# The first part of a gated DeltaNet mixer in another order: logit weights split earlier, decays behind the third convolution, convolutions apart from heads

## The chip, the core and the metric

One core of one Trainium2 chip runs the whole kernel in one launch. The metric is the device time of an execution in microseconds (us); a kernel's time is the median of its runs. The kernel before was run three times: 1945.94 us median, 1945.79 us lowest, 1953.51 us highest.

## What is computed

One inference step of a two-layer decoder trunk on 544 tokens: a prompt of 512 and eight samples of 4 tokens each, with shared weights, model width 1024, all in float32. Each layer is half an FFN, a mixer, half an FFN, each behind an RMS norm and added to the residual. Layer 0 mixes with stick-breaking attention and an RG-LRU; layer 1, the "odd" one, is a gated DeltaNet with 8 heads of width 128. Only the odd mixer matters here:

```python
def deltanet_mixer(u, conv_buf, S0, w_in, conv_w, A_log, dt_bias, o_gain, w_out):
    proj = u @ w_in                                   # 1024 -> q, k, v, z (1024 each), 8 + 8 logits
    qkv, z, b_logit, a_logit = jnp.split(proj, ...)
    qkv, new_buf = causal_conv(conv_buf, qkv, conv_w) # width 4, per channel
    q, k, v = jnp.split(jax.nn.silu(qkv), 3, axis=-1)
    q = l2_normalize(q) * (DN_HEAD_DIM ** -0.5); k = l2_normalize(k)
    beta = jax.nn.sigmoid(b_logit)
    g = -jnp.exp(A_log) * jax.nn.softplus(a_logit + dt_bias)
    o, S = gated_delta_chunked(q, k, v, beta, g, S0)  # G = cumsum(g); decay = exp(G_i - G_j); A = k k^T * decay * beta; ...
    o = rms_norm(o, o_gain) * jax.nn.silu(z)
    return o @ w_out, (new_buf, S)
```

## The kernel before

**Linear layers.** The activations lie feature-major, 128 features on the partitions and 544 tokens along the free axis, in two halves of 256 and 288 columns. Every linear layer (`mm3`, L347) is made of float32r matmuls: weights and activations are each split into a high and a low part and three products are added up (L362 to L364), so one 128-column tile of weights over 1024 inputs takes 48 matmuls for both halves. The weights of such a tile (class `W`, L304) come by one DMA of 512 KB on SyncE's queue (L319) into `raw` (two buffers); ScalarE rounds it to `wh` (L323, three buffers), VectorE subtracts to get `wl` (L324, two buffers). The product stands in a PSUM bank of tag `lin`, of which the odd mixer has two; the bank comes free when VectorE has read it (L1068 for the first half of a convolution, L1071 and L1072 for the second).

**Which order counts.** The Python code traces the instructions in one order, and a planner of the tile framework gives each engine its fixed order at build time: of the instructions that its own cost model holds to be ready, the one traced first. Each engine's queue then runs in that order on the chip, whatever comes late. The tokens of `ODD_ORDER` (L903) set the traced order of the odd mixer.

**Where layer 1's FFN meets the mixer.** `ffn_body` ends with eight feature tiles; behind each of them `split_x` makes the mixer's inputs `xh` (ScalarE, L267) and `xl` (VectorE, L268) and adds up the squares (`xsq`, L271 and L273). The weights that come next are loaded and split meanwhile. `mid` is a hook between the two linear layers of the FFN, in which `odd_consts` (L945) loads the mixer's constants.

**The start of the mixer.** `norm_stats` makes `rstd`, the tokens' scale (L280 to L289). `odd_setup` (L984) takes the 16 columns of logit weights as one more `W`, multiplies (48 matmuls, 16 output rows), scales the two halves by `rstd` into `bt` (L991), transposes them to tokens (L995), computes beta and the decays in many small steps (softplus with ScalarE's exponential at L100, five small matmuls L1018 to L1022, running sums `G`), writes `G` to DRAM (L1050, L1051) and reads it back as rows that are repeated on every partition (`grs` L1053; `grow`, and in `xsq` for the odd head, L1108).

**Heads.** The heads go in four groups of two. Token D (`decays`) makes for both heads of a group the two decay matrices `Dn` and `Dt`: 16 VectorE instructions of 128 x 128 (L1113, L1114) and their exponentials on ScalarE. Token H (`head_stage`, L1122) makes a head's q and k with `conv_tile` (L1056: linear layer, a scaled copy on ScalarE L1080, three multiply-adds on VectorE L1082, SiLU on ScalarE), then transposes (L1132, L1138), squares (L1134, L1140) and the products k k^T and q k^T (L1151, L1159) that the decays weight (L1153, L1160). These four PSUM results are of tag `m`, which has two banks. Token B makes v with a third `conv_tile`, Z the gate, V, L, S, C, R the inverse, the chunks' chain and the samples, O and M the output layer.

**Function tables.** ScalarE's exponential and its SiLU lie in different table sets. `E.table` (L86) issues a load of the other set where the set changes (L91) and orders it behind every traced use of the last set and ahead of every use of the next. Copies and squares are bound to no set.

```python
ODD_ORDER = "D0 H0 H1 B0 B1 V0 Z0 L0 Z1 S0 C0 R0 D2 H2 B2 H3 B3 ..."
...
    qT = conv_tile(E, op, w_in, 0, h, sq)      # in head_stage
    kT = conv_tile(E, op, w_in, 1, h, sq)
...
        norm_stats(E)                          # in odd_mixer
        odd_setup(E, cp, op, w_in)
        odd_heads(E, op, dp, w_in, w_out, nxt)
```

Of the kernel before, what the change touches and what calls it, by code (L numbers as in the profile page):

```python
# [15 lines left out]
P = 128  # L16
D = 1024
# [58 lines left out]
class Env:  # L76
# [75 lines left out]
def fetch_vectors(E, part):  # L152
    """Small vectors as rows of 128: the norms' gains, or the rest."""
# [46 lines left out]
def fetch_x(E, io, first):  # L200
    """The tokens' rows on their way, the norms' gains among them."""
# [13 lines left out]
def load_x(E, gname):  # L215
    """x feature-major and its split parts, the first half of the tokens ahead of the second."""
# [27 lines left out]
def store_tile(E, m, y, ys):  # L244
    """The output's columns of one feature tile, by way of the rows y and ys."""
# [58 lines left out]
class W:  # L304
    """Weight rows ks (of 128) by some columns, at most 8 blocks of 128 x 128, split in two exact float32r parts."""
# [22 lines left out]
    def part(self, c0, cn):  # L328
        """The columns c0 and on alone."""
# [5 lines left out]
def wide(E, src, ks):  # L335
    """Weight rows ks, all columns: a list of 128-column parts, each made when it is asked for."""
# [10 lines left out]
def mm3(E, ws, xh, xl, evac, ks=None, halves=(0, 1)):  # L347
    """psum[cols, half] = W^T x with three exact products."""
    nc = E.nc
    for h in halves:  # L350
# [8 lines left out]
        for i, (w, k) in enumerate(terms):  # L359
# [4 lines left out]
            nc.tensor.matmul(ps[:n], lhsT=wl, rhs=rh, start=False, stop=(i == len(terms) - 1))  # L364
# [67 lines left out]
def softplus_exp(E, pool, x, n):  # L432
    """exp(-|x|), the part of softplus that takes ScalarE's exponential."""
# [6 lines left out]
def softplus_log(E, pool, out, x, e, n):  # L440
    """out = softplus(x) = max(x, 0) + log1p(e), e = exp(-|x|), the logarithm by the series of atanh."""
# [21 lines left out]
def even_consts(E, cp):  # L463
# [36 lines left out]
    # gather rows of the pages in reverse: pool row page * 128 + 127 - p, four row parts each  # L500
# [54 lines left out]
def lru_gate_weights(E):  # L555
    """The gates' 64 x 64 blocks, two of them on the diagonal of each [128, 128]; exact float32r parts."""
# [103 lines left out]
def to_tokens(E, src, dst, sdst, dram, sdram, p):  # L660
    """Feature-major [128, NT] to token rows, kept in dst / sdst and stored."""
# [49 lines left out]
def page(E, ap, name, o):  # L711
    """A page of the cache, its rows in reverse."""
# [6 lines left out]
def sample_scores(E, ap, qb, ks, zs, hf):  # L719
    """q k of the sample's heads, rows (b in 4, head, token): 256 past keys in reverse, then the new ones."""  # L720
# [23 lines left out]
def sample_weights(E, ap, zs):  # L744
# [13 lines left out]
    for hf in range(2):  # L758
        nc.vector.tensor_tensor_scan(t[:, hf, :256], E.ones256, m[:, hf, :256], tot[:, hf:hf + 1], op0=ALU.mult, op1=ALU.add)
# [143 lines left out]
ODD_ORDER = "D0 H0 H1 B0 B1 V0 Z0 L0 Z1 S0 C0 R0 D2 H2 B2 H3 B3 Z2 Z3 V2 L2 D4 S2 C2 R2 H4 H5 B5 D6 Z4 B4 V4 Z5 H6 S4 H7 B6 L4 V6 C4 R4 B7 Z6 O0 Z7 N L6 C6 S6 R6 M2 O6"  # L903
# [21 lines left out]
def rsqrt_small(E, out, m, shape, tag):  # L925
    """out = m^-1/2 on a few columns: a first guess from the exponent, then Newton's steps."""
# [13 lines left out]
def bc(ap, n):  # L940
    """[p, a] -> [p, a, n], the last dimension repeated."""
# [3 lines left out]
def odd_consts(E, op):  # L945
# [14 lines left out]
    # conv weights and states, channels on partitions  # L960
# [17 lines left out]
    E.ogain = gc  # L978
    E.ad = op.tile([P, 2, NH], F32, name="ad")
# [63 lines left out]
    # the decays as rows, by way of DRAM, repeated on every partition  # L1043
# [12 lines left out]
def conv_tile(E, op, w_in, i, h, sq):  # L1056
    """Linear, causal convolution and SiLU of one 128-channel tile; the sample's tokens go to sq."""
# [23 lines left out]
    for j in range(1, 4):  # L1081
        nc.vector.scalar_tensor_tensor(a, XP[:, j:j + XW - 3], cw[j], a, op0=ALU.mult, op1=ALU.add)  # L1082
# [21 lines left out]
def head_decay(E, op, h):  # L1104
# [17 lines left out]
def head_stage(E, op, w_in, h, H, ssq, adr, sq):  # L1122
    """Everything of a head that does not need the inverse."""
# [3 lines left out]
    qT = conv_tile(E, op, w_in, 0, h, sq)  # L1127
    kT = conv_tile(E, op, w_in, 1, h, sq)
# [78 lines left out]
def levels(E, op, Hs, tdr):  # L1207
    """The transposed inverses of the 128 x 128 blocks of a group from those of their 32 x 32 blocks."""
# [430 lines left out]
```

## Time and profile before

| | us |
|---|---|
| runs: median, lowest, highest | 1945.94, 1945.79, 1953.51 |
| profiled execution, first to last instruction (span) | 1943.3 |
| median of the runs less that span | 2.6 |
| TensorE busy in the span | 1899.1 (98%) |
| VectorE busy | 1066.3 (55%) |
| ScalarE busy | 824.0 (42%) |
| mean granted TensorE clock | 0.989 |
| layer 1's odd mixer, from its first matmul | 1215.6 on |

The profiled execution has no run time of its own among the runs shown; its span is 2.6 us under their median, which holds the start and end of an execution that the span leaves out. Times in the rows are us from the span's start. The granted clock is a share of the full 2.4 GHz: 1.00 is 2.4 GHz, 0.50 is 1.2 GHz. "Busy" of PE (TensorE) is modelled for pipelined matmuls, so a busy PE may still be slow; where matmuls follow each other, the distance of their starts is what one costs. A wait names the instruction that ended it.

### The profile page before, as it was taken

The numbers are of one execution on the slowest core, as the hardware profiler recorded it, in microseconds if no ns is written. First come the engines' busy times: TensorE is split into PE (matmuls) and PEld (weight loads), VectorE is DVE, ScalarE is ACT, GpSimd is POOL, SyncE is SP. The second block draws the span as 40 slices with busy tenths as digits, with TensorE's granted clock in tenths as the row PEclk, the third lists the DMA queues.
The fourth block names the chain that finished last, engine by engine and source line by source line (L and its number), as shares of the span: only waits on it lengthen the run. The fifth ranks groups of instructions, "written<-read, shape, count | busy, mean of one in ns | idle before, by whom it ended". The sixth has DMA issues, their size and how long they took to land.

```text
span 1943.3 us, 36239 instructions
## 1 busy us (share of the span) xinstructions
PE 1899.1 (98%) x14905; PEld 1803.1 (93%) x14905; DVE 1066.3 (55%) x2544; ACT 824.0 (42%) x1709; POOL 110.9 (6%) x222
## 2 busy tenths in 40 slices
PE   7999999999999999999999999899999999999999
PEld 7999999879667999999999999799998998999998
DVE  7444335566755544433544433787968868444422
ACT  6333224667653433322433322566665636333221
POOL 0000001001221000000000000112110100000000
PEclk9999999999999999999999999999998999999999
DMA  4333233222323333323333323333343322333332
GB/s 132 87 88 88 80 90 98 78 55 84 93 84 91 88 87 87 88 83 88 99 88 87 88 80 79 88 96 92 92 108 86 92 79 69 87 88 88 88 110 67
DMA packets 313857, 171.00 MB, mean 88 GB/s; under 512 B 24310, under 2 KB 308166, under 8 KB 313692
## 3 DMA queue, kind: packets, MB, share of 16 engines
q1 hardware_dynamic: 311132, 160.30, 29.5%
q0 software_dynamic: 2560, 8.39, 1.5%
q8 instruction: 117, 1.92, 0.4%
q14 instruction: 48, 0.39, 0.1%
HBM read 158.01 MB, written 10.65 MB: 87 GB/s over the span
## 4 chain that ended last, share of the span: by engine, by line
PE 87%; DVE 5%; ACT 3%; issue 2%; DMA 2%; POOL 1%; SPq 0%; ACTq 0%; DVEq 0%; POOLq 0%
PE lin L362 25%; PE lin L363 25%; PE lin L364 25%; PE pv L707 1%; PE z L685 1%; DVE wl L324 1%; PE s L1421 1%; PE sc L736 1%; ACT wh L323 1%; PE po L783 0%; DMA raw<-in_w_ffn_in 0%; DVE acc L1082 0%; DVE ltmp L1199 0%; PE m L590 0%; ACT xh L267 0%
## 5 line engine op out<-in xcount | busy, mean ns | idle before, releaser
L362 PE MATMUL lin<-xh,wh 128*128 128x256 f32 (+2 forms) x2992 | 875.2, 293 | 18.5 <-DVE x L1532 4.2
L363 PE MATMUL lin<-xl,wh 128*128 128x256 f32 (+2 forms) x2992 | 872.8, 292 | 0.3 <-DVE xl L268 0.2
L364 PE MATMUL lin<-xh,wl 128*128 128x256 f32 (+2 forms) x2992 | 868.6, 291 | 1.2 <-DVE wl L324 1.2
L362 PEld LDWEIGHTS lin<-xh,wh 128*128 128x128 f32 (+1 forms) x2992 | 567.0, 190 | 25.3 <-ACT wh L323 6.4
L364 PEld LDWEIGHTS lin<-xh,wl 128*128 128x128 f32 (+1 forms) x2992 | 568.2, 190 | 9.2 <-issue 6.3
L363 PEld LDWEIGHTS lin<-xl,wh 128*128 128x128 f32 (+1 forms) x2992 | 567.4, 190 | 4.9 <-issue 2.3
L323 ACT ACTIVATE wh<-raw 128x1024 fp32r<-128x1024 f32 x261 | 275.6, 1057 | 507.5 <-PE lin L363 432.6
L324 DVE TENSOR_TENSOR wl<-raw,wh 128x1024 fp32r<-128x1024 f32 x261 | 317.2, 1215 | 89.6 <-PE lin L364 88.0
L362 PE MATMUL lin<-hh,wh 128*128 128x288 f32 (+1 forms) x1024 | 295.7, 289 | 0.0
L363 PE MATMUL lin<-hl,wh 128*128 128x288 f32 (+1 forms) x1024 | 295.4, 288 | 0.0
L364 PE MATMUL lin<-hh,wl 128*128 128x288 f32 (+1 forms) x1024 | 294.9, 288 | 0.0
L363 PEld LDWEIGHTS lin<-hl,wh 128*128 128x128 f32 x1024 | 193.0, 188 | 0.2
L364 PEld LDWEIGHTS lin<-hh,wl 128*128 128x128 f32 x1024 | 192.7, 188 | 0.1
L362 PEld LDWEIGHTS lin<-hh,wh 128*128 128x128 f32 x1024 | 192.5, 188 | 0.1
L401 DVE TENSOR_TENSOR sg<-lin,rstd 128x256 f32<-128x256 f32 (+1 forms) x128 | 55.9, 438 | 161.9 <-PE lin L364 161.9
L406 DVE TENSOR_TENSOR pr<-lin,rstd 128x256 f32<-128x256 f32 (+1 forms) x128 | 56.5, 441 | 155.3 <-PE lin L364 155.1
L370 ACT ACTIVATE hh<-pr 128x256 fp32r<-128x256 f32 (+1 forms) x128 | 55.1, 431 | 203.3 <-DVE pr L407 203.0
L423 DVE SCALAR_TENSOR_TENSOR x<-lin,x 128x256 f32<-128x256 f32 x64 | 28.2, 441 | 168.8 <-PE lin L364 168.8
L371 DVE TENSOR_TENSOR hl<-pr,hh 128x256 fp32r<-128x256 f32 (+1 forms) x128 | 56.6, 442 | 61.5 <-ACT hh L370 61.5
L100 ACT ACTIVATE sg<-sg 128x256 f32<-128x256 f32 (+1 forms) x128 | 53.7, 422 | 55.9 <-DVE sg L401 55.9
L267 ACT ACTIVATE xh<-x,vec 128x544 fp32r<-128x544 f32 (+2 forms) x64 | 39.6, 632 | 71.9 <-DVE x L423 59.6
L1082 DVE SCALAR_TENSOR_TENSOR acc<-XP,cw,acc 128x568 f32<-128x568 f32 x72 | 58.7, 816 | 3.9 <-ACT acc L1080 3.6
(474 smaller groups left out, 2056.4 us busy)
## 6 DMA issues: line engine op xcount, KB each, us to landing
raw<-in_w_ffn_in SPq DMA_DIRECT2D x128, 512.0 KB
raw<-in_w_ffn_out SPq DMA_DIRECT2D x64, 512.0 KB
raw<-in_w_in_odd SPq DMA_DIRECT2D x32, 512.0 KB
raw<-in_w_in_even SPq DMA_DIRECT2D x20, 512.0 KB
raw<-in_w_out_even SPq DMA_DIRECT2D x8, 512.0 KB
S<-in_state_dn_S SPq DMA_DIRECT2D x8, 512.0 KB
out_dn_S_sample<-S SPq DMA_DIRECT2D x8, 512.0 KB
raw<-in_w_out_odd SPq DMA_DIRECT2D x8, 512.0 KB
```

The lines of the kernel that those rows point to most:

```text
L100: i = self.nc.scalar.activation(out, in_, func, **kw).ins
L267: nc.scalar.activation(xh, x, AF.Copy, scale=g)
L323: nc.scalar.activation(self.h, raw, AF.Copy)
L324: nc.vector.tensor_tensor(self.l, raw, self.h.bitcast(F32), op=ALU.subtract)
L362: nc.tensor.matmul(ps[:n], lhsT=wh, rhs=rh, start=(i == 0), stop=False)
L363: nc.tensor.matmul(ps[:n], lhsT=wh, rhs=rl, start=False, stop=False)
L364: nc.tensor.matmul(ps[:n], lhsT=wl, rhs=rh, start=False, stop=(i == len(terms) - 1))
L370: nc.scalar.activation(yh, src, AF.Copy)
L371: nc.vector.tensor_tensor(yl, src, yh.bitcast(F32), op=ALU.subtract)
L401: nc.vector.tensor_tensor(s, ps, E.rstd[:, c0:c0 + cn], op=ALU.mult)
L406: nc.vector.tensor_tensor(p_, ps, E.rstd[:, c0:c0 + cn], op=ALU.mult)
L1082: nc.vector.scalar_tensor_tensor(a, XP[:, j:j + XW - 3], cw[j], a, op0=ALU.mult, op1=ALU.add)
```

## The change

Five things change; comments and docstrings that the diff also removes are left out here.

1. The logit weights are no longer a `W` of the mixer. `odd_consts` loads and splits them in the FFN's `mid` into tiles of their own (`w16`), so they take no `raw`, `wh` and `wl` buffer.
2. `odd_setup` is cut in two. `odd_logits` (the 48 matmuls and `bt`) stays at the start. The rest is token Y behind the first convolution; its first transpose is ordered behind the last matmul traced before it (`E.last_mm`, of q0).
3. Convolutions have tokens of their own: q0, k0, q1 and k1 are traced apart from H0 and H1, as "q0 Y k0 q1 D0 k1 H0 H1"; every other head takes its convolutions in its H token as before.
4. The first `Dn` instruction of heads 0 and 1 is ordered behind the last multiply-add of the convolution traced before (q1).
5. `ones256` shrinks to 128 columns and the samples' scan (L759) reads one column repeated 256 times; of three scratch tiles `junk` two stay.

Tokens q, k, Y and D each call `E.table`, so the sets now follow each other as SiLU (q0), exponential (Y), SiLU (k0, q1), exponential (D0), SiLU (k1 and on), where before there was one change behind D0.

```diff
-    E.ones256 = E.cp.tile([P, 256], F32, name="ones256")
-    nc.vector.memset(E.ones256, 1.0)
-    ones = E.ones256[:, :P]
+    ones = E.cp.tile([P, P], F32, name="ones")
+    nc.vector.memset(ones, 1.0)
...
-            nc.tensor.matmul(ps[:n], lhsT=wl, rhs=rh, start=False, stop=(i == len(terms) - 1))
+            E.last_mm = nc.tensor.matmul(ps[:n], lhsT=wl, rhs=rh, start=False, stop=(i == len(terms) - 1)).ins
...
-        nc.vector.tensor_tensor_scan(t[:, hf, :256], E.ones256, m[:, hf, :256], tot[:, hf:hf + 1], op0=ALU.mult, op1=ALU.add)
+        nc.vector.tensor_tensor_scan(t[:, hf, :256], E.ones[:, :1].to_broadcast([P, 256]), m[:, hf, :256], tot[:, hf:hf + 1], op0=ALU.mult, op1=ALU.add)
...
-ODD_ORDER = "D0 H0 H1 B0 B1 V0 Z0 L0 ...
+ODD_ORDER = "q0 Y k0 q1 D0 k1 H0 H1 B0 B1 V0 Z0 L0 ...
...
+    E.w16 = object.__new__(W)                                   # in odd_consts
+    raw = E.f()[:, :16 * KD].rearrange("p (k c) -> p k c", k=KD)
+    nc.sync.dma_start(out=raw, in_=w_in[:, 4096:4112].rearrange("(k p) c -> p k c", p=P))
+    E.w16.h, E.w16.l = (op.tile([P, KD, 16], F32R, name=n) for n in ("wh16", "wl16"))
+    split_to(E, E.w16.h, E.w16.l, raw)
+    E.w16.at = {k: k for k in range(KD)}
...
-def odd_setup(E, op, sp, w_in):
-    w = W(E, w_in[:, 4096:4112])
+def odd_logits(E, sp):
+    nc = E.nc
     bt = sp.tile([P, 4 * GH, P], F32, tag="V", name=E.nm("bt")).rearrange("p a b -> p (a b)")[:, :NT]
     def ev(h, c0, cn, ps):
         nc.vector.tensor_tensor(bt[:16, c0:c0 + cn], ps[:16], E.rstd[:16, c0:c0 + cn], op=ALU.mult)
-    mm3(E, [w], E.xh, E.xl, ev)
+    mm3(E, [E.w16], E.xh, E.xl, ev)
+    return bt
+
+def odd_setup(E, op, sp, bt):
     ps = E.m([P, 5, 16])
     for t, (c0, n) in enumerate(TOKS):
-        nc.tensor.transpose(ps[:n, t], bt[:16, c0:c0 + n], E.ident[:16, :16])
+        i = nc.tensor.transpose(ps[:n, t], bt[:16, c0:c0 + n], E.ident[:16, :16]).ins
+        if t == 0:
+            E.after(i, E.last_mm)
...
-        nc.vector.scalar_tensor_tensor(a, XP[:, j:j + XW - 3], cw[j], a, op0=ALU.mult, op1=ALU.add)
+        E.last_conv = nc.vector.scalar_tensor_tensor(a, XP[:, j:j + XW - 3], cw[j], a, op0=ALU.mult, op1=ALU.add).ins
...
-        nc.vector.scalar_tensor_tensor(Dn[:, c], ch(grow)[:, c], g, E.mba, op0=ALU.subtract, op1=ALU.max)
+        i = nc.vector.scalar_tensor_tensor(Dn[:, c], ch(grow)[:, c], g, E.mba, op0=ALU.subtract, op1=ALU.max).ins
+        if h < GH and c == 0:
+            E.after(i, E.last_conv)
...
-    qT = conv_tile(E, op, w_in, 0, h, sq)                       # head_stage now gets qT and kT
-    kT = conv_tile(E, op, w_in, 1, h, sq)
...
+    bt = odd_logits(E, op)                                      # in odd_heads
+
+    def linear(i, h):
+        g0 = h // GH * GH
+        if g0 not in st:
+            st[g0] = H = Group()
+            H.sq = op.tile([P, GH, 3, NS], F32, tag="sq", name=E.nm("sq"), bufs=2)
+        if (i, h) not in conv:
+            E.table("silu_and_others")
+            conv[i, h] = conv_tile(E, op, w_in, i, h, st[g0].sq)
+        return conv[i, h]
...
+        qT, kT = linear(0, h), linear(1, h)                     # in head(h)
+        head_stage(E, op, h, H.hs[h % GH], qT, kT, H.ssq, H.adr)
...
+        if c == "q":
+            linear(0, i)
+        elif c == "k":
+            linear(1, i)
+        elif c == "Y":
+            E.table(LNEXP)
+            odd_setup(E, cp, op, bt)
```

## Rows read from the trace of the kernel before

**Rows 1.** The page's first part, the whole span: busy time, share and instructions of each engine.

```profile
PE 1899.1 (98%) x14905; PEld 1803.1 (93%) x14905; DVE 1066.3 (55%) x2544; ACT 824.0 (42%) x1709; POOL 110.9 (6%) x222
```

**Rows 2.** The view of waits, PE alone, 1215 to 1262 us: who waited for whom, us in total, times, longest.

```profile
PE lin L362 <- DVE XP L1068: 3.7, 1, 3.7
PE m L995 <- DVE bt L991: 2.0, 1, 2.0
PE lin L362 <- ACT xh L267: 0.7, 1, 0.7
```

**Rows 3.** The table by stretches at the mixer's start: length, busy time and instructions of PE, PEld, DVE, ACT and POOL, granted clock, DMA share, GB/s. The sum is over the five stretches.

```profile
1223.50:1225.60 2.10, 0.14 (x2) 0.05 (x1) 1.91 (x6) 1.44 (x3) 0.00 (x0) 1.00 0.00 0
1225.60:1246.30 20.70, 20.70 (x160) 19.78 (x160) 15.92 (x56) 5.20 (x13) 3.82 (x8) 1.00 0.46 111
1246.30:1250.00 3.70, 0.00 (x0) 0.00 (x0) 3.70 (x13) 3.50 (x6) 0.00 (x0) 0.84 0.01 4
1250.00:1255.00 5.00, 4.96 (x23) 5.00 (x24) 2.71 (x8) 3.36 (x7) 3.18 (x5) 0.50 0.31 70
1255.00:1262.00 7.00, 6.96 (x52) 6.49 (x51) 4.93 (x15) 5.18 (x23) 0.57 (x3) 0.95 0.22 67
sum 38.50, PE 32.77 PEld 31.30 DVE 29.17 ACT 18.67 POOL 7.57; mean PE 6.55 PEld 6.26 DVE 5.83 ACT 3.73 POOL 1.51
```

**Rows 4.** The chain that ended last, in order of time, 1215 to 1262 us: start, length, what. Each piece released the next.

```profile
1212.96 4.10 DMA raw<-in_w_in_odd
...
1218.22 0.64 ACT xh L267
...
1225.10 0.42 DVE bt L991
...
1239.13 5.39 DMA grow<-gdr
1244.54 0.35 DVE Dn L1113
...
1248.83 0.72 DVE acc L1082
1249.55 0.34 DVE XP L1068
```

**Rows 5.** PE's timeline: start, length of one or of a merged run, line, out<-in, and in brackets the idle time before it. q0's first matmul; first, second and last of the 48 of q1; two of k1; then the first of head 0's own work, its transposes of q.

```profile
1225.78 0.39 PE L362 MATMUL lin<-xh,wh 128*128 128x256 f32 x1
...
1240.11 0.28 PE L362 MATMUL lin<-xh,wh 128*128 128x256 f32 x1
1240.23 0.28 PE L363 MATMUL lin<-xl,wh 128*128 128x256 f32 x1
...
1246.01 0.29 PE L364 MATMUL lin<-xh,wl 128*128 128x288 f32 x1
...
1250.60 0.41 PE L364 MATMUL lin<-xh,wl 128*128 128x256 f32 x1
1250.81 0.41 PE L362 MATMUL lin<-xh,wh 128*128 128x256 f32 x1
...
1254.87 0.99 PE L1132 MATMUL m<-ident,acc 128*128 128x128 f32 x4
```

**Rows 6.** VectorE's timeline, same columns: the low part of the logit weights, the last update of the FFN's last feature tile, the low part of q0's weights, and q1's three multiply-adds in one merged row.

```profile
1212.60 0.29 DVE L324 TENSOR_TENSOR wl<-raw,wh 128x128 fp32r<-128x128 f32 x1 [2.77 <-PE lin L364]
1215.80 0.46 DVE L423 SCALAR_TENSOR_TENSOR x<-lin,x 128x288 f32<-128x288 f32 x1 [2.91 <-PE lin L364]
1216.18 1.22 DVE L324 TENSOR_TENSOR wl<-raw,wh 128x1024 fp32r<-128x1024 f32 x1
...
1256.96 2.50 DVE L1082 SCALAR_TENSOR_TENSOR acc<-XP,cw,acc 128x568 f32<-128x568 f32 x3 [0.33 <-ACT acc L1080]
```

**Rows 7.** ScalarE's timeline, same columns: k0's weights, the first exponential of softplus, the last exponential of the setup, the last of the decays and the table load behind it, then SiLU of q0 and, last row, of k1.

```profile
1217.16 1.06 ACT L323 ACTIVATE wh<-raw 128x1024 fp32r<-128x1024 f32 x1 [3.58 <-DMA raw<-in_w_in_odd]
...
1227.82 0.24 ACT L100 ACTIVATE spe<-spe 128x40 f32<-128x40 f32 x1
...
1235.53 0.24 ACT L100 ACTIVATE egl<-egl 128x40 f32<-128x40 f32 x1 [0.35 <-DVE egl L1036]
...
1250.07 0.62 ACT L100 ACTIVATE xsq<-xsq 128x512 f32<-128x512 f32 x1
1250.69 1.28 ACT L91 ACT_TABLE_LOAD   x1
1251.98 0.63 ACT L100 ACTIVATE acc<-acc 128x512 f32<-128x512 f32 x1
...
1267.74 0.63 ACT L100 ACTIVATE acc<-acc 128x512 f32<-128x512 f32 x1 [0.84 <-DVE acc L1082]
```

**Rows 8.** Four source lines over the whole span, L91 (table loads), L759 (the samples' scan), L1071 (a convolution's second half out of its bank) and L1080 (its scaled copy): count, shortest/median/longest in ns, first and last start.

```profile
L91 ACT ACT_TABLE_LOAD  x19: 1283/1283/1283, 0.7 to 1653.5; - x19
...
L759 DVE TENSOR_TENSOR_SCAN tm<-ones,tot,tm x2: 726/738/751, 567.7 to 568.4; 128x256 f32<-128x256 f32 x2
...
L1071 DVE TENSOR_TENSOR XP<-lin,rstd x24: 405/419/428, 1232.6 to 1528.4; 128x256 f32<-128x256 f32 x24
...
L1080 ACT ACTIVATE acc<-XP,cw x24: 752/758/773, 1233.4 to 1531.2; 128x568 f32<-128x568 f32 x24
```

**Rows 9.** The table by stretches, columns as in Rows 3, for one later stretch of the mixer.

```profile
1380.00:1400.00 20.00, 18.19 (x147) 17.01 (x145) 19.27 (x85) 15.29 (x43) 4.01 (x9) 1.00 0.23 57
```

More of the change, by code (lines that the diff above doesn't have):

```diff
@@ L902 @@
 XW = 3 + T + DB * 7
-ODD_ORDER = "D0 H0 H1 B0 B1 V0 Z0 L0 Z1 S0 C0 R0 D2 H2 B2 H3 B3 Z2 Z3 V2 L2 D4 S2 C2 R2 H4 H5 B5 D6 Z4 B4 V4 Z5 H6 S4 H7 B6 L4 V6 C4 R4 B7 Z6 O0 Z7 N L6 C6 S6 R6 M2 O6"
+ODD_ORDER = "q0 Y k0 q1 D0 k1 H0 H1 B0 B1 V0 Z0 L0 Z1 S0 C0 R0 D2 H2 B2 H3 B3 Z2 Z3 V2 L2 D4 S2 C2 R2 H4 H5 B5 D6 Z4 B4 V4 Z5 H6 S4 H7 B6 L4 V6 C4 R4 B7 Z6 O0 Z7 N L6 C6 S6 R6 M2 O6"
 def odd_const_arrays():
@@ L942, in bc, with odd_consts @@
     return ap.unsqueeze(2).to_broadcast([ap.shape[0], ap.shape[1], n])
-def odd_consts(E, op):
+def odd_consts(E, op, w_in):
     nc, I = E.nc, E.I
@@ L1119, in head_decay, with head_stage @@
     return H
-def head_stage(E, op, w_in, h, H, ssq, adr, sq):
+def head_stage(E, op, h, H, qT, kT, ssq, adr):
     nc = E.nc
@@ L1358, in sample_group @@
     for h in hs:
-        nc.scalar.activation(E.junk[2][:NS], kt[:, h], AF.Square, accum_out=ssk[:, h:h + 1])
+        nc.scalar.activation(E.junk[1][:NS], kt[:, h], AF.Square, accum_out=ssk[:, h:h + 1])
     nc.vector.tensor_scalar(ssk, ssk, EPS, None, op0=ALU.add)
@@ L1473, in odd_mixer @@
         E.ft, E.rt = (op, "acc", XW, 4), (op, "y", YB)
-        E.junk = [op.tile([P, P], F32, name=f"junk{i}") for i in range(3)]
+        E.junk = [op.tile([P, P], F32, name=f"junk{i}") for i in range(2)]
         E.svz = op.tile([NS, GH, 2, NS], F32, name="svz")
@@ L1477, in odd_mixer, with odd_heads @@
         norm_stats(E)
-        odd_setup(E, cp, op, w_in)
-        odd_heads(E, op, dp, w_in, w_out, nxt)
-def odd_heads(E, op, dp, w_in, w_out, nxt):
+        odd_heads(E, cp, op, dp, w_in, w_out, nxt)
+def odd_heads(E, cp, op, dp, w_in, w_out, nxt):
     nc, tc, O = E.nc, E.tc, E.O
-    st, Y = {}, {}
+    st, Y, conv = {}, {}, {}
+    bt = odd_logits(E, op)
[8 more added lines that the diff above has]
+        return conv[i, h]
     def decays(g0):
         E.table(LNEXP)
-        st[g0] = H = Group()
-        H.sq = op.tile([P, GH, 3, NS], F32, tag="sq", name=E.nm("sq"), bufs=2)
+        if g0 not in st:
+            st[g0] = Group()
+        H = st[g0]
+        if not hasattr(H, "sq"):
+            H.sq = op.tile([P, GH, 3, NS], F32, tag="sq", name=E.nm("sq"), bufs=2)
         H.ssq = op.tile([P, GH, 4], F32, tag="ssq", name=E.nm("ssq"), bufs=2)
@@ L1498, in head @@
         E.table("silu_and_others")
-        head_stage(E, op, w_in, h, H.hs[h % GH], H.ssq, H.adr, H.sq)
+        qT, kT = linear(0, h), linear(1, h)
+        head_stage(E, op, h, H.hs[h % GH], qT, kT, H.ssq, H.adr)
     def gate(h):
@@ L1551, in odd_heads @@
         H = st.get(i // GH * GH)
-        if c == "D":
+        if c == "q":
[5 more added lines that the diff above has]
+            odd_setup(E, cp, op, bt)
+        elif c == "D":
             decays(i)
@@ L1618, in build @@
         with tc.tile_pool(name="odc", bufs=1) as cp:
-            ffn(E, *f[1][0], ("norm_mix", 1), mid=lambda: odd_consts(E, cp))
+            ffn(E, *f[1][0], ("norm_mix", 1), mid=lambda: odd_consts(E, cp, I["w_in_odd"][0]))
             odd_mixer(E, cp, I["w_in_odd"][0], I["w_out_odd"][0], ("norm_ffn2", 1))
```

## The prediction

> **What bounds the kernel now.** I read the page first: TensorE is busy for 98% of the span [rows 1], so only a change of PE's own work or a stretch in which it stands still or runs slowly can move the time. The change leaves its matmuls as they are in number and size, so I looked for the stretches. The view of waits, for PE alone around the mixer's start, shows three [rows 2]: 3.7 us on the first half of a convolution leaving its bank, 2.0 us on `bt`, 0.7 us on `xh`. The table by stretches shows them in place [rows 3]: PE has 0.14 of 2.10 us before q0, then is full for 20.7 us, then empty for 3.7 us, and behind that stop it runs the next 5 us at a granted clock of 0.50 (1.2 GHz). The price of the slow clock is in the distance of PE's starts [rows 5]: 0.12 us at full clock (1240.11 to 1240.23), 0.21 behind the stop (1250.60 to 1250.81); 23 matmuls [rows 3] at 0.09 more are 2.1 us.
>
> The chain of waits says why [rows 4]. The 3.7 us: the rows of running decays land at 1244.5 (a DMA of 5.39 us), VectorE then makes the 16 instructions of D0 without a break, one multiply-add of k0's convolution and only then the evacuation for which PE waits, 1249.55. The reader should see that q1's first half had long been multiplied: D0 stood ahead of it in VectorE's queue because it is traced earlier. The 2.0 us hang on a chain that begins with the DMA of a weight tile, 1212.96 for 4.10 us. ScalarE waited 3.58 us for it before k0's `wh` [rows 7], and the last `xh` came behind that at 1218.2, then sums, `rstd` and `bt` at 1225.1 [rows 4].
>
> **The change, part by part.** The sum is made against the profiled span, 1943.3 us; I take the 2.6 us between it and the median of the runs as unchanged.
>
> *Decays behind the third convolution.* q1 gets out of its banks ahead of D0, so PE goes from q1 straight to k1. It takes away 3.7 us of standing still [rows 2] and the 2.1 us of slow clock behind it: -5.8.
>
> *Logit weights out of the rotation.* Every weight load moves one place forward: k0's comes where q0's came and has landed long before 1212.96. What of the wait before k0's `wh` remains depends on the planner. Best end: `xh` starts when the last update ends, 1215.80 + 0.46 = 1216.3 [rows 6], instead of 1218.2, but `xl` stays behind a `wl` that ends at 1217.4 [rows 6], so `bt` comes 1.5 earlier. Worst end: q1's `wh` takes k0's place ahead of `xh`. Its load is released by q0's `wl`, which moves to 1212.60 and takes 1.22 where the logits' took 0.29 [rows 6], so it lands 0.9 later than 1217.06, and all is 0.9 later. No row lies nearer to one end; I take the middle, -0.3. The split itself (one instruction of 0.29 on VectorE [rows 6], one like it on ScalarE, one DMA on SyncE's queue) moves into the FFN, where PE is behind neither; without that cover 0.6.
>
> *The setup behind q0 (token Y).* Its transposes and small matmuls cost PE the same as before: 20.7 us of full PE [rows 3] less three convolutions of 6.0 (1240.11 to 1246.01 + 0.13 [rows 5]) leave 2.6 for them. 0. What Y does to the decays is a matter of time. Behind q0, now up at about 1225.5 + 6.0 = 1231.5, come evacuation 0.6, copy 0.76 [rows 8], multiply-adds 2.50 [rows 6], SiLU 0.85 (0.63 and a small one like the setup's last, 0.24 [rows 7]) and a table load 1.28 [rows 8]: Y's first exponential starts at 1237.5 where it started at 1227.8 [rows 7]. With everything behind it as long as before, the decays' rows land 9.7 later, 1254.2, D0 ends on VectorE at 1258.5 (4.3 for it [rows 4]) and on ScalarE at 1260.4, and k1's SiLU follows behind a table load at 1261.7. Before, it stood at 1267.7 [rows 7]. So head 1 is not held up: 6 us of slack.
>
> *Convolutions apart from heads.* PE's list is then q0, k0, q1, k1, 24.0 + 2.6 from 1225.5, until about 1252.1. Then comes head 0's own work, 3.9 us (12.0 from k1's start to 1262, less 6.0 and 2.1 [rows 3, 5]); its q and k are through SiLU by then. Two of its products must wait in the two `m` banks until D0 is through, some 4 us; meanwhile PE has v of head 0, another 6.0. 0, with 2.5 as the worst, if PE's fixed order has a third user of an `m` bank ahead of that filler.
>
> *Table loads.* Four more at 1.28 [rows 8], 5.1 us on ScalarE, which has 18.67 of 38.5 us here [rows 3]: hidden, 0; their delays stand in the two items before. The trace shows the load of rows 7 begin as the last exponential ends (1250.07 + 0.62) and SiLU start 1.29 later, so 1.28 is all that a switch costs. The Trainium skill speaks against this change here: its page "ScalarE: Activation LUTs", under "What ACT_TABLE_LOAD costs", adds a drain of about 1.38 us to each load, 2.66 in all, and under "Rules for kernel authors" asks to finish one set before the next. By that page the decays would come 1.4 later and k1's SiLU 5.5 later, at an estimated 1267.2, still not behind the old time; it would only make the first rival dearer. The trace's load without a drain does not bear the page out.
>
> *The scan over a repeated column.* Two instructions of 0.74 [rows 8]; they write as many elements as before, 0; twice as long would be 1.5, and nothing speaks for less. One scratch tile less is used by one engine in its own order: 0.
>
> Sum: -5.8 - 0.3 = -6.1. The span becomes 1937.2, the time **1939.8**.
>
> **Rivals.**
> 1. *The stop comes back behind k1, and longer.* Decision: does k1's evacuation stand behind D0 in VectorE's queue? D0 is traced ahead of it, as it was ahead of q1. Then PE waits from 1252.1 until the rows land (1254.2), D0 (4.3), a multiply-add (0.7) and the evacuation (0.4) are done: 7.5, and 2.1 of slow clock, 9.6 against 6.1 won: **1949.4**; if head 0's 3.9 can fill part of it, 1945.5. For it: the planner did just this with q1. Against it: k1's first half is through PE at about 1249, five us before the rows land, where q1's was through 1.5 before.
> 2. *Only the named instructions move.* One `Dn` of each head is bound, the other 14 of D0 are not. If the planner puts those ahead of q1's evacuation, the old stop stays: 1945.6. Against it: the rows now land some 8 us behind q1's last matmul.
> 3. *The lead is not kept.* PE is ahead by 6 us, but later places are VectorE's: of 20 us from 1380 it is busy 19.27, PE 18.19 [rows 9]. Were the 1.8 that PE loses there lost at two places more, 3.6 of the lead would go: 1943.4. Against it: VectorE has done the same work by then and has spare time where PE now stands still.
> 4. *More than the stop.* The opening at its best end (1.2 more) and the wait from 1380 dissolved by the new packing (1.8), with 0.7 for the opening's `xh` wait: 1936.1.
>
> **How the numbers follow.** The forecast gets 0.55, own range 1937 to 1943 (the ends of the opening, the 2.5 of the `m` banks); rival 3 0.20, rival 1 0.12, rival 2 0.05, rival 4 0.08. The range 1935 to 1949.5 takes in all four and leaves out the tails. A measurement of this kernel can tell about 0.5%, 9.7 us, from no change: faster needs under 1936.2, which rival 4 gives and the forecast hardly, 0.09; slower needs over 1955.7, rival 1 twice over or a second such stop downstream, 0.05; the rest, 0.86, is the same. All that PE loses at this start is 8.5 us, so little more than 0.4% is to be had.
>
> **What would show it.** Right: no wait of PE on a convolution's evacuation near 1246, clock 1.00 through the first four convolutions, four in a row before head 0's transposes; 23 table loads in the page's rows; the first exponential of softplus some 10 us behind its old place without a wait of PE. Opening: the last `xh` at 1216.3 or 1219. Wrong: PE empty behind k1 with the evacuation behind D0 (rival 1), `Dn` rows ahead of q1's multiply-adds (rival 2), new PE waits after 1280 that together come near 6 us (rival 3).

## The result and the profile after

The changed kernel takes 1974.72 us (median of 4 runs, 1971.35 to 1975.99); the kernel before, on the same chip, 1949.09 us (4 runs, 1945.79 to 1953.51). The ratio is 1.0131, 95% interval 1.0104 to 1.0158: 26 us slower, where 6 us faster was forecast. The profiled execution took 1975.99 us with a span of 1974.2. The mixer's lines of the changed kernel stand some 13 behind those of before (L1068 is L1081, L1080 is L1093, L1156 is L1169, L1193 is L1206), earlier lines one ahead (L362 is L361).

**The start went as forecast.** The page's first part (compare [rows 1]) and PE's waits from 1215 to 1262 us (compare [rows 2]):

```profile
PE 1915.6 (97%) x14905; PEld 1816.6 (92%) x14905; DVE 1065.8 (54%) x2544; ACT 830.9 (42%) x1713; POOL 108.0 (5%) x222
```

```profile
PE lin L361 <- DVE bt L996: 1.3, 1, 1.3
PE m L282 <- ACT r L279: 0.4, 1, 0.4
```

The wait of 3.7 us is gone. The table by stretches (columns as in [rows 3]; the last stretches lie behind those of rows 3 and are discussed below):

```profile
1246.30:1250.00 3.70, 3.70 (x29) 3.28 (x28) 2.74 (x8) 0.00 (x0) 0.25 (x2) 1.00 0.58 142
1250.00:1255.00 5.00, 5.00 (x42) 4.87 (x42) 2.58 (x11) 4.42 (x10) 1.66 (x3) 1.00 0.09 13
1255.00:1262.00 7.00, 7.00 (x57) 6.79 (x57) 5.56 (x16) 6.16 (x25) 0.54 (x3) 1.00 0.68 166
1262.00:1270.00 8.00, 5.80 (x35) 5.34 (x34) 7.82 (x32) 6.68 (x14) 2.10 (x3) 0.79 0.19 45
...
1380.00:1400.00 20.00, 11.66 (x74) 9.45 (x73) 16.41 (x83) 15.53 (x44) 0.39 (x1) 0.74 0.24 70
...
1640.00:1660.00 20.00, 15.70 (x67) 13.63 (x67) 9.46 (x35) 6.16 (x18) 0.39 (x1) 0.53 0.00 0
```

PE is full at clock 1.00 from 1246 to 1262, where it stood still and then ran at 0.50 before. Behind that it does worse. First it stands for a product of head 0 whose `m` bank ScalarE has not yet emptied: the copy of the transposed keys (L1154) starts at 1263.53, behind three exponentials of D0 (waits, 1262 to 1270):

```profile
PE m L1172 <- ACT kt L1154: 1.4, 1, 1.4
```

And where it was busy 18.19 of 20 us from 1380 [rows 9], it is busy 11.66, at 0.74.

**The decays came later than forecast.** Three pieces of the chain that ended last (compare [rows 4]):

```profile
1214.68 4.21 DMA raw<-in_w_in_odd
...
1254.59 5.38 DMA grow<-gdr
1259.99 0.35 DVE Dn L1126
```

The load of the decays' rows starts at 1254.59 instead of 1239.13: 15.5 us later. ScalarE's timeline shows how that begins (SiLU of q0, table load, first exponential of softplus, last of the setup, table load, SiLU of k0; then the load and the SiLU of k1; compare [rows 7]), and the line of table loads is the one that answers to [rows 8]:

```profile
1235.79 0.63 ACT L100 ACTIVATE acc<-acc 128x512 f32<-128x512 f32 x1 [2.80 <-DVE acc L1095]
...
1236.55 1.28 ACT L91 ACT_TABLE_LOAD   x1
...
1238.09 0.22 ACT L100 ACTIVATE spe<-spe 128x40 f32<-128x40 f32 x1
...
1251.15 0.24 ACT L100 ACTIVATE egl<-egl 128x40 f32<-128x40 f32 x1 [0.30 <-DVE egl L1049]
1251.40 1.28 ACT L91 ACT_TABLE_LOAD   x1
1252.69 0.63 ACT L100 ACTIVATE acc<-acc 128x512 f32<-128x512 f32 x1
...
1265.74 1.28 ACT L91 ACT_TABLE_LOAD   x1
1267.04 0.63 ACT L100 ACTIVATE acc<-acc 128x512 f32<-128x512 f32 x1
```

```profile
L91 ACT ACT_TABLE_LOAD  x23: 1283/1283/1283, 0.7 to 1683.4; - x23
```

The exponential of softplus is 10.3 us late, as foreseen. The other 5 us are lost behind it, on VectorE (timeline, compare [rows 6]):

```profile
1245.86 0.20 DVE L450 SCALAR_TENSOR_TENSOR sps<-sps,sps 128x40 f32<-128x40 f32 x1
1245.99 0.80 DVE L1095 SCALAR_TENSOR_TENSOR acc<-XP,cw,acc 128x568 f32<-128x568 f32 x1
1246.71 0.19 DVE L452 SCALAR_TENSOR_TENSOR g<-sps,g 128x40 f32<-128x40 f32 x1
1246.82 0.81 DVE L1095 SCALAR_TENSOR_TENSOR acc<-XP,cw,acc 128x568 f32<-128x568 f32 x1
...
1249.89 0.19 DVE L1043 COPY G<-m 128x32 f32<-128x32 f32 x1 [0.96 <-PE m L1035]
```

In the kernel before, the same copy of G stands here:

```profile
1234.08 0.19 DVE L1030 COPY G<-m 128x32 f32<-128x32 f32 x1 [0.94 <-PE m L1022]
```

From the exponential to G it was 6.3 us (1227.82 to 1234.08) and is 11.8 (1238.09 to 1249.89): the setup's steps of 0.2 us each now alternate with a convolution's of 0.8. Six multiply-adds, of k0 and q1, and two weight splits of 1.2 us stand among them; before, none did.

**What hangs on that date.** The queue of SyncE, before and after: A of head 0 and of head 1 stored, then loaded for the solve of group 0.

```profile
1265.97 1.77 SPq L1156 DMA_DIRECT2D adr<-Dn  x4
...
1278.61 1.74 SPq L1156 DMA_DIRECT2D adr<-Dn  x4
...
1281.59 1.72 SPq L1193 DMA_DIRECT2D LA<-adr  x4
```

```profile
1272.92 1.77 SPq L1169 DMA_DIRECT2D adr<-Dn  x4
...
1285.18 1.74 SPq L1169 DMA_DIRECT2D adr<-Dn  x4
1288.26 1.71 SPq L1206 DMA_DIRECT2D LA<-adr  x4
```

The solve of group 0 starts 6.7 us later (1288.26 for 1281.59). Not all that follows is later (A of the third head is stored at 1324.99, for 1327.88 before), but the solves are: group 2's by 9.0 us, group 4's by 18.1, group 6's by 13.6 (1545.46 for 1531.83).

**Where the time went.** I cut the stretch from 1215.6 to the last table load (a mark at the end of the mixer: 1653.45 before, 1683.36 after) into pieces of 4 us and took two losses from each: the part in which PE is not busy, and busy time x (1 - granted clock). What is left, work at full clock, is 399 to 405 us in all kernels of this study, so the two losses carry nearly all of the difference. In us, not busy + slow clock:

| stretch | before | after | e1 | e2 | e3 | e4 | e5 | e10 |
|---|---|---|---|---|---|---|---|---|
| 1215.6 to 1262 | 6.6+2.6 | 2.6+0 | 1.6+0 | 6.5+3.1 | 2.5+0 | 4.7+1.4 | 2.2+0 | 4.6+0 |
| 1262 to 1300 | 1.4+0 | 2.1+1.4 | 3.1+1.5 | 1.4+0 | 0.5+1.2 | 1.5+0 | 3.9+0 | 3.5+3.4 |
| 1300 to 1400 | 2.1+3.4 | 12.0+11.0 | 11.4+7.3 | 2.4+1.7 | 10.0+11.3 | 2.4+1.7 | 11.5+7.8 | 14.8+13.4 |
| 1400 to 1500 | 3.4+8.2 | 3.5+10.2 | 3.7+10.5 | 3.1+8.1 | 1.9+3.4 | 3.8+1.7 | 2.9+3.4 | 1.1+6.0 |
| 1500 to 1600 | 1.3+3.4 | 3.8+0 | 2.5+3.4 | 1.2+0 | 1.8+3.4 | 2.4+10.4 | 2.8+3.4 | 1.8+3.4 |
| 1600 to the mark | 4.9+0 | 9.6+10.6 | 4.5+11.7 | 9.4+9.6 | 3.7+1.6 | 4.2+4.6 | 4.6+1.4 | 4.6+5.1 |
| sum | 37 | 67 | 61 | 46 | 41 | 39 | 44 | 62 |

The start gives back 6.6 us, as forecast (6.1). It is paid back nearly three times over from 1300 to 1400 (17.5 us more) and once more in the last stretch (15.3 more). The last stretch has a cause of its own. On ScalarE the samples of group 6 have their transposed keys at 1558, and their squares run 70 us later, directly behind the last squares of the chain:

```profile
1558.31 0.59 ACT L1368 ACTIVATE skv<-s 32x512 f32<-32x512 f32 x1 [1.05 <-PE s L1366]
...
1627.85 0.29 ACT L1324 ACTIVATE junk<-ot 128x128 f32<-128x128 f32 x1
...
1628.27 0.31 ACT L1372 ACTIVATE junk<-skv 32x128 f32<-32x128 f32 x1
```

Before, they ran at 1566:

```profile
1566.27 0.29 ACT L1359 ACTIVATE junk<-skv 32x128 f32<-32x128 f32 x1
```

Both squares write a tile that nobody reads. It was `junk[2]` for the samples and is `junk[1]` now, the chain's; the chain of group 6 (C6) is traced ahead of its samples (S6), so the second write waits for the first.

### The profile page after: what moved, and what is told of

Its sections match the earlier page's. It is cut to its first block, busy times and chain, and to the rows that moved or that the text cites. A ratio compares the mean times of both kernels' runs of the same rounds, so it can differ in the third digit from the quotient of the medians.

```text
span 1974.2 us, 36246 instructions
## 1 busy us (share of the span) xinstructions
PE 1915.6 (97%) x14905; PEld 1816.6 (92%) x14905; DVE 1065.8 (54%) x2544; ACT 830.9 (42%) x1713; POOL 108.0 (5%) x222
## 4 chain that ended last, share of the span: by engine, by line
PE 84%; DVE 5%; DMA 3%; issue 3%; ACT 3%; POOL 1%; SPq 0%; ACTq 0%; DVEq 0%; POOLq 0%
PE lin L361 25%; PE lin L362 24%; PE lin L363 24%; PE pv L706 1%; PE z L684 1%; PE s L1434 1%; DVE wl L323 1%; PE sc L735 1%; DMA raw<-in_w_in_odd 1%; DMA raw<-in_w_ffn_in 1%; ACT wh L322 1%; DMA V<-tdr 1%; DVE acc L1095 0%; PE po L782 0%; DVE ltmp L1212 0%
## 5 line engine op out<-in xcount | busy, mean ns | idle before, releaser
L361 PE MATMUL lin<-xh,wh 128*128 128x256 f32 (+2 forms) x2992 | 877.1, 293 | 19.9 <-DVE f L647 3.5
L362 PE MATMUL lin<-xl,wh 128*128 128x256 f32 (+2 forms) x2992 | 874.6, 292 | 0.2 <-DVE xl L267 0.2
L361 PEld LDWEIGHTS lin<-xh,wh 128*128 128x128 f32 (+1 forms) x2992 | 567.4, 190 | 27.3 <-DVE XP L1081 3.8
L362 PEld LDWEIGHTS lin<-xl,wh 128*128 128x128 f32 (+1 forms) x2992 | 568.4, 190 | 4.4 <-issue 2.3
L361 PE MATMUL lin<-hh,wh 128*128 128x288 f32 (+1 forms) x1024 | 295.7, 289 | 0.0
L362 PE MATMUL lin<-hl,wh 128*128 128x288 f32 (+1 forms) x1024 | 295.4, 288 | 0.0
L362 PEld LDWEIGHTS lin<-hl,wh 128*128 128x128 f32 x1024 | 193.0, 188 | 0.2
L361 PEld LDWEIGHTS lin<-hh,wh 128*128 128x128 f32 x1024 | 192.5, 188 | 0.1
L406 DVE TENSOR_TENSOR pr<-pr,sg 128x256 f32<-128x256 f32 (+1 forms) x128 | 56.0, 438 | 6.8 <-DVE pr L405 0.5
```

The lines of the kernel that those rows point to most:

```text
L361: nc.tensor.matmul(ps[:n], lhsT=wh, rhs=rh, start=(i == 0), stop=False)
L362: nc.tensor.matmul(ps[:n], lhsT=wh, rhs=rl, start=False, stop=False)
L406: nc.vector.tensor_tensor(p_, p_, sg[:, c0:c0 + cn], op=ALU.mult)
```

## Experiments

Two theories of the loss: **the date** (the decays' rows land 15 us later, the mixer's serial part with them, and TensorE's linears, already used up, can't fill the gap) and **the tile** (the last group's samples wait for its chain). The rivals are in each expectation. All ratios are to the kernel before, run again on the same chip (its medians there: 1946.85 to 1948.28 us), with 95% intervals. They are not quotients of the medians given, which differ from them by up to 0.24% (1.0096 for e1), so smaller differences between kernels are uncertain in size.

**e1: the tile back.** The samples' squares get a target of their own; the rest of the change stays.

```
+    kw = R(P, "kw")
...
-        nc.scalar.activation(E.junk[1][:NS], kt[:, h], AF.Square, accum_out=ssk[:, h:h + 1])
+        nc.scalar.activation(kw[:, h], kt[:, h], AF.Square, accum_out=ssk[:, h:h + 1])
...
-    kw = R(P, "kw")
```

> The changed kernel, but the samples' squares are written to a tile of their own again (the rows of kw, which are rewritten later by an instruction that needs the squares' sums anyway). Tile theory: in the changed kernel the squares of the samples' group 6 are ordered behind the chain's last squares, since both write junk[1]; with a tile of their own they run again soon after the transposed keys are there (skv, about 1558), the state of samples 6 is stored near 1610 to 1620 and not at 1662.6, the slow clock at 1640 to 1670 goes, and the whole takes 1963 us (1958 to 1968); the delay ahead of group 6 (the first group's inverse 11.8 us late) stays. Rival A (the decays' date alone): the tail is only the end of a late mixer, and the time stays at 1972 to 1976. Rival B (the tile is all of it): back to 1949.

Measured: 1966.91 us (7 runs), ratio 1.0072 (1.0047 to 1.0097). The squares run at 1557.6 again (`skw` is their new target):

```profile
1557.56 0.31 ACT L1373 ACTIVATE skw<-skv 32x128 f32<-32x128 f32 x1
```

The delay ahead of group 6 stays (its solve starts at 1544.16). Neither rival's figure fits. The tile accounts for 0.59 of the 1.31% (0.22 to 0.96; both kernels against the kernel before; 0.36 by the medians), the rest is left for the date. The seven runs spread from 1957.95 to 1970.36; the profiled one, of 1970.1, is among the longest, and the 11.7 us of slow clock in the last row of its column are that execution's.

**e2: the tile alone, in the kernel before.**

```
-        nc.scalar.activation(E.junk[2][:NS], kt[:, h], AF.Square, accum_out=ssk[:, h:h + 1])
+        nc.scalar.activation(E.junk[1][:NS], kt[:, h], AF.Square, accum_out=ssk[:, h:h + 1])
```

> The kernel before, with that alone changed: the samples' squares write junk[1], as the chain's do. Tile theory: the samples of group 6 wait for the chain's last squares, run by themselves at the end with little beside them, and the whole takes 1959 us (1955 to 1966); nothing moves ahead of 1560. Rival A (decays' date alone): 1949, as before, since the last group's chain is early enough. Rival B (all of the loss): 1972 or more.

Measured: 1957.21 us (10 runs), ratio 1.0036 (1.0019 to 1.0054): 7 us for one index. ScalarE's timeline and the stretch behind it:

```profile
1607.90 0.31 ACT L1311 ACTIVATE junk<-ot 128x128 f32<-128x128 f32 x1
...
1608.33 0.31 ACT L1359 ACTIVATE junk<-skv 32x128 f32<-32x128 f32 x1
```

```profile
1620.00:1640.00 20.00, 15.96 (x64) 13.85 (x63) 9.37 (x37) 7.11 (x22) 0.39 (x1) 0.50 0.00 0
```

In the same stretch of the kernel before:

```profile
1620.00:1640.00 20.00, 15.61 (x114) 14.09 (x112) 18.10 (x54) 12.40 (x30) 0.00 (x0) 1.00 0.16 47
```

The busy time is alike, the number of matmuls is 64 against 114: the samples run by themselves, at 1.2 GHz, and PE has nothing else to do.

**e9: the tile shared, the samples traced first.**

```
-... N L6 C6 S6 R6 M2 O6"
+... N L6 S6 C6 R6 M2 O6"
```

> The changed kernel with the tile still shared, but with the last group's samples written ahead of its chain (L6 S6 C6 R6 for L6 C6 S6 R6). Tile theory: what costs is the order in which the two writers of the shared tile stand, not the sharing; with the samples first their squares run near 1558 again, the chain's squares behind them find the tile free, and the time is that of e1, 1966 us (1962 to 1970). Rival (any sharing costs, or the last group's chain is held up by the samples in its turn): 1973 or more.

Measured: 1959.2 us (8 runs), ratio 1.0060 (1.0041 to 1.0079). The squares run at 1565:

```profile
1565.12 0.31 ACT L1372 ACTIVATE junk<-skv 32x128 f32<-32x128 f32 x1
```

So sharing is harmless and the order of the two writers costs; that tracing the samples first gains nothing by itself, in the old order at least, is shown by e11 below. That the time is even below the interval forecast is within what e1 leaves open.

**e3: the setup ahead of the first convolution**, otherwise e1.

```
-"q0 Y k0 q1 D0 k1 H0 H1 ...
+"Y q0 k0 q1 D0 k1 H0 H1 ...
```

> As e1, and the setup of the decays stands directly behind the logits, ahead of the first convolution (Y q0 k0 q1 D0 k1); the decays of group 0 still wait for the third convolution. Theory of the date (mixer's end follows the date of the decays' rows): the first exponential comes back to about 1228, the rows land near 1250, where they were 1260 in the changed kernel, and 9 to 12 us of the mixer come back: 1952 us (1948 to 1956) if e1 gives 1963. Rival A (convolutions put ahead use up the linear work that filled TensorE later, whatever the decays do): no change against e1. Rival B (the three convolutions' DVE work still holds D0 back, to the third convolution's end): half of it, 1957.

Measured: 1947.61 us (10 runs), ratio 0.9995 (0.9976 to 1.0014). One token's place is worth 0.77% (0.46 to 1.08), 15 us; more than the 9 to 12 expected, and the rival that the convolutions ahead are all of the cost is out: they are still ahead. The exponential and the rows' load stand within 1.1 us of where they stood before:

```profile
1228.88 0.24 ACT L100 ACTIVATE spe<-spe 128x40 f32<-128x40 f32 x1
```

```profile
1239.88 0.46 SPq L1121 DMA_DIRECT2D grow<-gdr  x1
...
1280.99 2.36 SPq L1169 DMA_DIRECT2D adr<-Dn  x4
...
1284.60 1.71 SPq L1206 DMA_DIRECT2D LA<-adr  x4
```

The last two rows are A of head 1 and the solve of group 0: 4.2 and 3.7 us earlier than in the changed kernel, for rows that are loaded 14.7 earlier. A of head 0 is no earlier (1273.48 for 1272.92): most of D0 still stands behind the third convolution and ends on VectorE at 1255.8, where it ended at 1248.8 in the kernel before.

The table adds two things. From 1300 to 1400 e3 loses 21.3 us, as the changed kernel does (23.0), though its rows are early. But its first solve is still 3.0 us later than in the kernel before, and that date sorts all kernels of this study: the eight whose first solve starts at 1284.6 or later lose 19 to 28 us in this stretch, the six in which it starts at 1282.2 or earlier lose 4 to 9. (That is an order of dates seen afterwards and not an experiment; of the eight, e10 alone has the old order.) What e3 does better than e1 comes behind it: 5.3 for 14.2 us from 1400 to 1500, and 5.3 for 16.2 in the last stretch. And e3 has the whole gain of the start (2.5 for 9.2 us) and is still no faster than the kernel before: that gain does not reach the end.

**e5: e3 with late rows.** Moving a token moves more than one thing, so this delays the rows alone.

```
+    for j in range(6):
+        g2 = E.dp.tile([NH, NT], F32, name=f"gdr{j}")
+        nc.sync.dma_start(out=g2, in_=E.gdr)
+        E.gdr = g2
```

> As e3 (setup first, third convolution ahead of the decays), but the decays go through six more DRAM copies, one after the other, before their rows are loaded, so that these land some 16 us later, at about the changed kernel's date; nothing else is moved in the text. Theory of the date: the rows' lateness alone brings the loss back, 1962 to 1968 us. Rival A (what costs in the changed kernel is that the setup's function set holds the second and third convolution's SiLU on ScalarE until 1255, the rows have slack): 1947 to 1952. Rival B (only the order of TensorE's linears, the same here as in e1, matters): it would be 1967 in both, which e3 has already refuted for itself, so 1948.

Measured: 1959.45 us (5 runs), ratio 1.0063 (1.0042 to 1.0083). The queue shows the copies, first and last, and the load behind them:

```profile
1239.45 3.99 SPq L1067 DMA_DIRECT2D gdr<-gdr  x2
...
1250.38 4.06 SPq L1067 DMA_DIRECT2D gdr<-gdr  x2
...
1256.69 1.33 SPq L1125 DMA_DIRECT2D grow<-gdr  x1
...
1289.90 1.71 SPq L1210 DMA_DIRECT2D LA<-adr  x4
```

The load is 16.8 us later than in e3, the solve 5.3, and the time 0.68% (0.40 to 0.96), 13 us: under the 14 to 20 forecast, but most of what e1 and e3 differ by. The SiLUs, which rival A blamed, are early here. The weights' loads share SyncE's queue with the copies, but the copies do not hold them up: they are issued at 1243.60, 1249.62 and 1255.65, in e3 at 1243.39, 1249.86 and 1257.46.

**e10: the old order with late rows.** As e4 below, with the same six copies.

> As e4 (weights split early, the order of the kernel before), with the six more DRAM copies of e5 ahead of the decays' rows, which land some 16 us later. Theory of the date: e5 lost about 12 us by 16, so here 1957 us (1953 to 1961). Rival A (the old order has room, the first two heads' linears and convolutions fill the wait): 1945 to 1949. Rival B (the decays on VectorE now stand in the middle of the heads' convolutions): 1962 or more.

Measured: 1968.84 us (4 runs), ratio 1.0104 (1.0073 to 1.0134), against e4 1.28% (0.92 to 1.64), 25 us, for a load at

```profile
1254.74 1.07 SPq L1125 DMA_DIRECT2D grow<-gdr  x1
```

instead of 1237.8. The date costs in this order too, and double what I expected: rival B's figure, and its mark is in the waits (PE, 1262 to 1300):

```profile
PE lin L361 <- DVE XP L1089: 3.9, 1, 3.9
PE lin L361 <- DVE XP L1085: 2.0, 1, 2.0
```

Both evacuations stand behind D0's sixteen steps on VectorE, as in the kernel before. The solve starts at 1292.98, 14.0 us later than in e4, where the same delay moved it by 5.3 in e5. With late rows the order with the convolutions apart (e5) is better than the old one; with early rows it is not (e3 against e4).

**e6: the setup later still**, behind q1, otherwise e1 ("q0 k0 q1 Y D0 k1").

> As e1, with the setup one step further back: q0 k0 q1 Y D0 k1. The first three convolutions' SiLU then run in one set of functions, ahead of the setup, near 1247 to 1252 instead of 1254 to 1256, and the decays' rows land 5 to 8 us later than in e1. Theory of the date: 1968 to 1976 us, later than e1's 1967 by a few us. Rival A (the held SiLUs are the cost): back towards e3, 1950 to 1957.

Measured: 1960.89 us (8 runs), ratio 1.0057 (1.0037 to 1.0077). The rows' load is at 1263.4, 7 us behind e1's, the solve 5.5 behind e1's (1295.63 for 1290.16), and the time is not above e1's. A miss: neither figure fits. The loss doesn't grow us by us with the date; all kernels with the convolutions ahead, a load between 1254 and 1264 and no late squares lie between 1.0057 and 1.0079 (e1, e5, e6, e7, e9), and the intervals of e1 and e6 overlap. That e6 has two table loads fewer than e1 (21 against 23) may be part of it; it isn't shown.

**e7: without the two written orders**, otherwise e1: both `E.after` lines of the change taken out.

> As e1, without the two orders that the change writes out (the transposes of the logits behind the last linear, group 0's decays behind the third convolution's last step); the order of the tokens stays q0 Y k0 q1 D0 k1. Theory of the date: in e1 the decays begin when their rows land, at 1262, long after the third convolution (1250), and the setup's first exponential waits for the first convolution's SiLU (1237.6) and not for the transposes (1233), so neither order binds: 1964 to 1968 us, as e1. Rival (the written orders are what makes the date late): 1950 to 1957.

Measured: 1965.5 us (4 runs), ratio 1.0079 (1.0053 to 1.0106), as e1. They cost nothing here that can be told.

**e4: the weights alone.** As e1 with the old order and no written order for the decays.

```
-"q0 Y k0 q1 D0 k1 H0 H1 ...
+"Y D0 H0 H1 ...
...
-        if h < GH and c == 0:
-            E.after(i, E.last_conv)
```

> As e1, but with the order of the kernel before (setup, decays, then each head with its two convolutions) and no wait of the decays for a convolution: what is left of the change is that the 16 columns of logit weights are loaded and split in the feed-forward layer, and the scan's ones. Theory of the date: the setup begins as early as before or 2 us earlier, nothing is late, and the time is 1947 us (1944 to 1950). Rival A (the split in the feed-forward layer itself costs, by its place on VectorE or by the order that it makes): 1953 or more. Rival B (the stop ahead of the first convolutions was worth all of its 5.8 us): 1943.

Measured: 1945.3 us (12 runs), ratio 0.9976 (0.9957 to 0.9996): 5 us (1 to 8) faster; 3 by the medians. The first part of the change costs nothing and is at most a small gain.

**Three attempts at more.** e8: e1 with "Y q0 k0 D0 H0 q1 k1 H1".

> A version that should keep both gains: the logit weights split early, the setup directly behind the logits, then the two convolutions of head 0, the decays of group 0 behind the second of them, head 0, and head 1 as before (Y q0 k0 D0 H0 q1 k1 H1). Theory of the date: the decays' exponentials end 3 to 5 us earlier than in e3, head 0's A is stored near 1266 instead of 1273, and the time is 1944 us (1941 to 1948). Rival A (the decays' sixteen steps on VectorE hold up the next linear's eviction again, as in the kernel before): 1948 to 1950. Rival B (the end of the mixer hangs on the later heads' linears, not on this date): 1947, as e3.

Measured: 1952.24 us (12 runs), ratio 1.0023 (1.0005 to 1.0041). A of head 0 was stored at 1263.4, even earlier than forecast, and from 1400 to 1500, far behind, PE is busy 90.60 of 100 us where in e4 it is 96.25:

```profile
1400.00:1500.00 100.00, 90.60 (x819) 85.34 (x818) 81.26 (x295) 59.23 (x173) 15.67 (x35) 0.97 0.38 97
```

e11: e4 with the last group's samples first, as in e9.

> As e4, with the last group's samples ahead of its chain (L6 S6 C6 R6). Theory: the end of the mixer is where TensorE has least to fill with; the samples' small steps then stand beside the chain instead of behind it, and the 9 us that e4 loses after 1600 shrink: 1941 us (1937 to 1945). Rival A (the planner puts them beside the chain in either case): 1945, as e4. Rival B (the samples delay the chain, which is the longer): 1949 or more.

Measured: 1945.95 us (12 runs), ratio 0.9979 (0.9961 to 0.9998), as e4: rival A.

e12: e4 with the first convolution alone ahead ("Y q0 D0 k0 H0 q1 k1 H1").

> As e4, with the first convolution alone moved ahead of the decays (Y q0 D0 k0 H0 q1 k1 H1), no written order. Theory of the date: the rows land as in e4, the decays' steps on VectorE come behind the first convolution's, which is done by then, TensorE's stop near 1246 shrinks by 1 to 3 us and head 0 is as early: 1943 us (1940 to 1947). Rival A (an order of later work that differs by chance, as in e8, whose loss came at 1400 to 1500, costs more than that): 1948 to 1953. Rival B (the stop stays): 1945.

Measured: 1944.6 us (12 runs), ratio 0.9978 (0.9959 to 0.9996), not to be told from e4. So e4, e11 and e12 are by their ratios about 0.2% faster than the kernel before (0.1% by the medians) and 1.5% faster than the changed one; that one of them is the best isn't shown.

## Why the prediction was wrong

- **The third-conv stop (-5.8) and the opening (-0.3): right.** Not busy and slow clock fell from 9.2 to 2.6 us up to 1262. `bt` came 0.5 earlier, near the forecast, but not by the middle way: `xh` started as the FFN's last update ended, the best end, and that update came 0.8 later than before (1216.57 for 1215.80); whether the split in the FFN did that isn't shown. Rivals 1 and 2 did not come: k1's evacuations, at 1248.53 and 1251.67, stand ahead of D0.
- **"Y's first exponential starts at 1237.5": right** (1237.84 for the first, beta's; 1238.09 for softplus').
- **"With everything behind it as long as before, the decays' rows land 9.7 later": failed.** 15.5. The steps behind the exponential took 11.8 us for 6.3, because VectorE runs them between the steps of convolutions, and of weight splits, ahead of which they used to stand. I priced where the setup begins and took its length from a stretch in which it had VectorE almost to itself.
- **"So head 1 is not held up: 6 us of slack": failed**, and it is the costliest step. k1's SiLU came at 1267.04, later than the 1261.7 forecast and still ahead of the old 1267.74, so the test that I set was passed. But it was the wrong test: the solve needs A of both heads, which needs the decays themselves. A of head 0 was stored 7.0 us later, A of head 1 6.6. I followed ScalarE's queue and not the path of the decays; e5 and e10 show that the rows' date costs 13 and 25 us when it alone is delayed by 17.
- **Convolutions apart 0: not borne out.** With the tile back, the date early and the start's gain in hand, e3 should by this sum be some 6 us faster than the kernel before; it is at 0.9995, at best 5 us faster (0.9976). In the changed kernel the wait of 1.4 us for an `m` bank, within the 2.5 that the prediction gave as the worst, came on top. In e3 the loss lies from 1300 to 1400, behind an A of head 0 that is as late as in the changed kernel, since D0 stands behind the third convolution.
- **Table loads 0.** e3 has two loads more than before and shows no cost that can be told apart from the item above. The two other loads of the change, around Y, belong to its place and weren't priced alone. By the drain that the Trainium skill ("ScalarE: Activation LUTs", "What ACT_TABLE_LOAD costs") adds to each load, the prediction estimated k1's SiLU at 1267.2, and it came at 1267.04; yet the rows show no drain, the load starts 0.01 us behind the last exponential (1251.15 + 0.24, 1251.40) and SiLU 1.29 us behind its start. The agreement is chance: the late decays made that date.
- **"One scratch tile less is used by one engine in its own order: 0": failed.** Being on one engine does not make it free: the order of two writes to one tile is that in which they are traced, so work that could run at 1558 stood behind work that ends at 1628. 0.36% by e2, 0.59% (0.22 to 0.96) by the step from the changed kernel to e1.
- **Rival 3, "the lead is not kept", had the right place**: the stretch from 1380 got worse. It was sized as two waits of 1.8 us; e3 shows that the lead is lost even with early decays, and no rival let the lateness of the decays run through the mixer.

What stays open: why 7 us at the first solve become 15 at the end (e1 against e3: 5.6 at the first solve, 15 at the end), and why e6, with a later solve than e1, is not slower. The loss from 1300 to 1400, which e1, e3 and e5 share, e3 makes good later; e8 loses far behind an earlier start. The planner lays the rest of the mixer out anew for each order, and which of the later waits follow from the date and which from that layout wasn't separated.

## What to carry to other kernels

When a step is moved, follow its result to the last consumer on the serial path and compare dates there; a queue in which nothing is late proves nothing about a path beside it. Price a chain of short steps by the company that it will have on its engine, not by its old length. A scratch output that nobody reads is still an order between its writers: when two uses come to share one, look at which of them the trace has first, above all at the end of a phase, where nothing fills the gap.

## What the runs showed of the hardware

- Small copies from DRAM to DRAM, each waiting for the one before, took 2.8 us each (e5: the first issued at 1239.45, the loads behind the sixth from 1256.06 on); four lines of code delayed a result by 17 us without taking a compute engine.
- TensorE's clock fell in e1's profiled execution without a stop in PE: from 1590 to 1636 it was busy throughout (46.00 of 46.00 us), and from 1612 to 1632 at the lower level (1.2 GHz) nearly all the time, with 32x32 matmuls of the levels among its work:

```profile
1612.00:1632.00 20.00, 20.00 (x150) 18.24 (x144) 10.57 (x37) 8.06 (x23) 0.39 (x1) 0.51 0.05 16
```

- Executions of one kernel differ by about as much as the effects looked for here, and their time goes with their mean clock: e4's twelve runs go from 1939.4 us at 0.991 to 1955.3 us at 0.983. A profile is one such execution, so a stretch of slow clock in it is not yet the kernel's.
